# Ten projections of a 1-core Trainium2 kernel: from channel-major matmuls of 256 columns to token-major matmuls of 512

## The chip, the cores and the metric

One Trainium2 chip, one core. The metric is device time in microseconds of one launch. Three runs of the kernel before gave 1682.53, 1684.06 and 1685.83 us; the median is 1684.06 us. The profiled execution, one more run, took 1684.61 us.

## The reference, cut to what matters

Two stacked networks work on 256 tokens of width 1024, batch 1, all in float32. The first has two layers of feed-forward, three-branch mixer, feed-forward. The second is one layer: a mixer of a gated delta rule beside an S5 state-space model, cross attention on 256 memory tokens, a feed-forward. The parts that the change touches are the inputs of channel-wise operations:

```python
# first network, state-space branch, in each of two layers
xbc = (h @ w_in[l])[..., 2208:3232]                # 1024 channels
xbc = silu(causal_conv4(xbc) + conv_b)             # along the tokens
xs, b_in, c_in = split(xbc, [512, 768])            # into the chunked scan
# second network, mixer
proj = rmsnorm(h) @ w_in
q, k, v = split(silu(causal_conv4(proj[..., :1536])), 3)   # 512 each
u = proj[..., 2056:2568]                           # 512, input of the S5 scan
o = gated_delta_rule(l2norm(q) * 128**-0.5, l2norm(k), v, g, beta)
y = s5(u)
# second network, cross attention
k_mem = rmsnorm(mem) @ w_xk                        # 1024 channels
```

## The kernel before

Tokens come in two halves of 128 (`t`), the width in eight tiles of 128 (`k`). A normed input is held transposed, features on partitions and 256 tokens along the free axis, as a pair: a rounded high part `hi` and the rest `lo`, both fp32r. Each float32 product is three matmuls, which `mac` (lines 284 to 288) issues: high by high, high by low, low by high. The row norm of the input (`r`, one value a token) is applied after the product.

Weights stream through `wload` (line 158): a DMA from the SyncE queue into one of five stage tiles of 128x1024 (`NS`), a ScalarE cast into one of four `whi` tiles (line 165), a VectorE subtraction into one of four `wlo` tiles (line 166, `NW`). These run at the highest priority (`WPRIO`). One such tile is 512 KB.

There are two forms of projection. `lin_tok` (line 290) is token-major: 128 tokens of the input are stationary, 512 weight columns move, and the output has tokens on partitions, in one PSUM bank for each token half. `lin_ft` (line 309) is channel-major: 128 weight columns are stationary, the 256 tokens move, and the output has channels on partitions. What needs channels on partitions (a convolution along the tokens, the S5 scan, the keys) comes from `lin_ft`:

- `channels` in `mixer1` (line 563, two layers): eight tiles of 128 channels in two groups of four. VectorE multiplies two of them at a time with `rrow`, the norms spread along the free axis (line 572). Then follow `conv` (line 474: ScalarE scaling, three VectorE steps a channel tile), tanh and one more step.
- `proj_ft` in `mixer2` (line 1238): the same for k, q, v (in this order, each with its convolution and SiLU) and u.
- `mem_kv` (line 1336): eight tiles of memory keys, evacuated by ScalarE, then the memory values with `lin_tok`.

`r_rows` (line 487) makes `rrow`: two TensorE transposes of a broadcast column and a ScalarE copy. It is called once in each `mixer1` and once in `mixer2`.

The feed-forwards (`ffn`, line 369) already turn a token-major product without TensorE, in `flip` (line 267). VectorE transposes 32x32 blocks of `hb` (line 273), four DMAs write the blocks to a DRAM tile in their new places (line 277, 64 KB each), one DMA reads it back (line 279, 256 KB), and `split_evac` (lines 188 and 189) makes the fp32r pair. The tile `hb` and the landing tile `flipped` have one buffer each, `flip` and the DRAM tile two.

The order on each engine is the tile framework's: it simulates the program on a cost model and takes ready instructions by priority, which is program order moved by the `high_priority` blocks. All DMAs are issued from SyncE in the order of that plan, and an instruction that waits holds up those behind it on its engine. In `mixer1` the steps come in the order of `SEQ` (line 36): x is `channels`, u the gated MLP, q the attention heads, z the state-space gate, S the scan, A the attention, then gates and branches. The scan and the attention have a raised priority. In `mixer2` the delta rule (`delta`, line 1036) stands ahead of its place by `DPRIO`; `s5_scan` (line 980) and `mem_kv` come after it in the program, `s5_scan` in four chunks of 128 channels of u. A gate projection of the scan's output (`gT`) follows, then `lin_out` with the outputs of both.

Of the kernel before, what the change touches and what calls it, by code (L numbers as in the profile page):

```python
# [8 lines left out]
F32 = mybir.dt.float32  # L9
F32R = mybir.dt.float32r  # L10
I32 = mybir.dt.int32
AF = mybir.ActivationFunctionType
# [54 lines left out]
class Net:  # L67
# [198 lines left out]

    def flip(self, src, n, hi, lo, t):


        nc = self.nc  # L270
        w = n * 32
        r = self.A([512], "flip")[:, :4 * w]
        nc.vector.transpose(r, src)
        d = self.dram.tile([P, 4 * w], F32, name="flips", tag="flips")
        to = d.rearrange("(j c) (i e) -> i c j e", c=32, e=w)
        for i in range(4):
            nc.sync.dma_start(out=to[i], in_=r[i * 32:i * 32 + 32].rearrange("p (j e) -> p j e", e=w))
        raw = self.A([512], "flipped")[:, :4 * w]
        nc.sync.dma_start(out=raw, in_=d)
        tok = slice(t * P, (t + 1) * P)  # L280
        hi, lo = [z[:, :, tok].rearrange("p k (a b) -> p k a b", b=32) for z in (hi, lo)]
        self.split_evac(raw.rearrange("p (a k b) -> p k a b", k=n, b=32), hi, lo)

# [25 lines left out]
    def lin_ft(self, xT, w, c, out):  # L309

        hi, lo = xT
        n = len(w)
        cc = slice(c * P, (c + 1) * P)
        for k in range(n):
            wh, wl = w[k]
            self.mac(out, wh[:, cc], wl[:, cc], hi[k], lo[k], k == 0, k == n - 1)

    def wcols(self, src, n):
# [50 lines left out]
    def ffn(self, norm, w_in, w_out, scale, nxt, aside=None):  # L369
        nc = self.nc  # L370
        xT, r = norm["xT"], norm["r"]
        hh, hl = [], []
        for c in range(6):
            n = 512 if c < 5 else 256
            th = self.A([4, S], "hTh", F32R)
            tl = self.A([4, S], "hTl", F32R)
            ps = self.lin_tok(xT, w_in[c * 8:c * 8 + 4], 512)
            if c < 5:
                pg, pu = ps, self.lin_tok(xT, w_in[c * 8 + 4:c * 8 + 8], 512)
            else:  # L380
                pg, pu = [[p[:, i * n:(i + 1) * n] for p in ps] for i in range(2)]
            for t in range(2):
                sg = self.A([512], "sg")
                nc.scalar.activation(sg[:, :n], pg[t][:, :n], AF.Silu, scale=r[t])
                hb = self.A([512], "hb")[:, :n]
                nc.vector.scalar_tensor_tensor(hb, pu[t][:, :n], r[t], sg[:, :n], ALU.mult, ALU.mult)
                self.flip(hb, n // P, th[:, :n // P], tl[:, :n // P], t)
# [98 lines left out]

    def r_rows(self, r, pool):

        p = self.tp()
        for t in range(2):  # L490
            self.row_bcast(r[t], p[:, t * P:(t + 1) * P])
        o = pool.tile([P, S], F32, name="rrow")
        self.nc.scalar.copy(o, p[:, :S])
        return o

    def mixer1(self, l, norm, nxt):
        nc, a = self.nc, self.a
        v, act, pe = nc.vector, nc.scalar, nc.tensor
        tt, stt, ts = v.tensor_tensor, v.scalar_tensor_tensor, v.tensor_scalar
        lay = self.lay = Arena(self, 3072, "lay1")  # L500
        xT, r = norm["xT"], norm["r"]
# [61 lines left out]
        def channels():  # L563

            rrow = self.r_rows(r, lay)
            for g in range(2):
                xb = self.A([4, S], "xb")
                for c2 in range(2):
                    p = self.mm()
                    for c in range(2):  # L570
                        self.lin_ft(xT, self.wcols(a["m1_xbc"][l][g * 4 + c2 * 2 + c][None], P), 0, p[:, c * S:(c + 1) * S])
                    tt(xb[:, c2 * 2:c2 * 2 + 2], self._shape(p, [2, S]),
                       rrow[:, None, :].to_broadcast([P, 2, S]), ALU.mult)
                d = self.A([4, S], "xc")
# [634 lines left out]
    def mixer2(self, norm, nxt):  # L1209
        nc, a = self.nc, self.a  # L1210
        v, act, pe = nc.vector, nc.scalar, nc.tensor
        tt, stt, ts = v.tensor_tensor, v.scalar_tensor_tensor, v.tensor_scalar
        lay = self.lay = Arena(self, 2560, "lay2")
        alog = self.row(a["dn_a_log"], 4, "alog2")
# [21 lines left out]
        rrow = self.r_rows(r, lay)  # L1236

        def proj_ft(src, dst):
            for i in range(src.shape[0] // 2):
                p = self.mm()  # L1240
                for c in range(2):
                    self.lin_ft(xT, self.wcols(src[i * 2 + c][None], P), 0, p[:, c * S:(c + 1) * S])
                tt(dst[i // 2][:, (i % 2) * 2:(i % 2) * 2 + 2], self._shape(p, [2, S]),
                   rrow[:, None, :].to_broadcast([P, 2, S]), ALU.mult)

# [33 lines left out]
        for i in (1, 0, 2):  # L1279
            xb = self.A([4, S], "xb2")  # L1280
            proj_ft(a["m2_qkv"][i * 4:i * 4 + 4], [xb])
            d = self.A([4, S], f"qkv{i}")
# [4 lines left out]
        uT = self.A([4, S], "uT")  # L1287
        proj_ft(a["m2_u"], [uT])

# [46 lines left out]
    def mem_kv(self, xT):  # L1336
        nc, a = self.nc, self.a
        self.xk = [self.A([4, S], "xk") for _ in range(2)]
        for i in range(4):
            p = self.mm()  # L1340
            for c in range(2):
# [120 lines left out]


def _out_w(w, cols=COLS):

# [16 lines left out]
def _prep(inp):  # L1482
# [15 lines left out]
    for l in range(2):  # L1498
        wl = w[l]
        cqw.append(_blk(wl, 1024, 384, 2))  # L1500
        ckvw.append(_blk(np.concatenate([wl[:, 1408:1696], wl[:, 3232:3240]], axis=1), 0, 296, 2))
        xbc.append(np.concatenate([_blk(wl, 2208 + P * i, P, 8) for i in range(8)]))
        zz.append(_blk(wl, 1696, 512, 2))
# [23 lines left out]
    w = inp["w_in_2"][0]  # L1527
    o["m2_u"] = np.concatenate([_blk(w, 2056 + P * i, P, 8) for i in range(4)])
    o["m2_qkv"] = np.concatenate([_blk(w, P * i, P, 8) for i in range(12)])
    o["m2_z0"] = _blk(np.concatenate([w[:, 1536:1792], w[:, 2048:2056]], axis=1), 0, 264, 2)  # L1530
# [27 lines left out]
    o["mem"] = inp["mem_2"].reshape(2, P, D)  # L1558
    for k in "qk":
        o["x_" + k] = np.concatenate([_blk(inp[f"w_x{k}_2"][0], P * i, P, 8) for i in range(8)])  # L1560
    o["x_v"] = np.concatenate([_blk(inp["w_xv_2"][0], 512 * i, 512, 2) for i in range(2)])
# [37 lines left out]
```

## Time and profile before

| | before |
|---|---|
| median of three runs | 1684.06 us |
| lowest and highest | 1682.53 and 1685.83 us |
| profiled execution, its own time | 1684.61 us |
| its span in the profile | 1682.7 us |
| TensorE busy, matmuls | 1662.7 us, 9222 |
| VectorE busy | 1133.0 us |
| ScalarE busy | 902.6 us |
| moved by DMA | 321.92 MB |

Times in the trace are counted from the start of the span. "PE" is TensorE's matmuls, "PEld" its weight loads, "DVE" is VectorE, "ACT" ScalarE, "SPq" the SyncE queue that issues DMAs. The duration of a matmul overlaps that of the next. "mm", "mmm" and "chs" are PSUM banks; "xh" and "xl" are the pair of the normed input, "memh" and "meml" that of the memory.

### The profile page before, as it was taken

Reading aid. Unit: us, or ns where it says so; the run is one execution under the profiler, and the core shown is the slowest. Engines: PE = TensorE matmul, PEld = TensorE weight load, DVE = VectorE, ACT = ScalarE, POOL = GpSimd, SP = SyncE. Lnnn points to the kernel's source line nnn. Section 1 sums busy time; section 2 is a strip of 40 time slices with the busy share of each in tenths; the row PEclk is TensorE's granted clock in tenths of the full one; section 3 lists DMA queues with packets and bytes.
Section 4 is the critical chain, followed back from the end, with each engine's and each line's share of the span. In section 5 each row is a group of like instructions: output and inputs, shape, how many; then the busy total and the mean of one; then the engine's idle time right before and its main releaser. Section 6 shows DMA issues by size and latency. Waiting matters only on the chain.

```text
span 1682.7 us, 24668 instructions
## 1 busy us (share of the span) xinstructions
PE 1662.7 (99%) x9222; PEld 1423.0 (85%) x9222; DVE 1133.0 (67%) x1840; ACT 902.6 (54%) x1361; POOL 78.6 (5%) x73
## 2 busy tenths in 40 slices
PE   8999999999999999999999999999999999999998
PEld 6888898888888888888988888888899888888888
DVE  5665598657666556665896666799689746755664
ACT  5444467564544444544666545545476555654443
POOL 0000013000000000000130000000010100000000
PEclk9999999999999999999999999999999999999999
DMA  7787556444677757786664545767764224347872
GB/s 257 242 241 246 180 187 188 156 141 132 199 245 248 232 175 239 251 237 187 206 191 144 161 145 190 231 202 233 237 197 141 64 63 154 123 150 237 262 241 99
DMA packets 132744, 321.92 MB, mean 191 GB/s; under 512 B 24592, under 2 KB 52752, under 8 KB 132624
## 3 DMA queue, kind: packets, MB, share of 16 engines
q1 hardware_dynamic: 132624, 320.35, 60.7%
q8 instruction: 72, 1.18, 0.3%
q14 instruction: 48, 0.39, 0.1%
HBM read 304.82 MB, written 15.47 MB: 190 GB/s over the span
## 4 chain that ended last, share of the span: by engine, by line
PE 96%; DVE 1%; ACT 1%; issue 0%; DMA 0%; POOL 0%; SPq 0%; POOLq 0%; DVEq 0%; ACTq 0%
PE mm L287 28%; PE mm L286 28%; PE mm L288 28%; PE tp L206 1%; PE mmm L286 1%; PE mmm L288 1%; PE mmm L287 1%; PE ch L752 1%; PE chs L999 1%; PE ch L774 1%; PE tp L263 1%; PE ch L1137 0%; PE tp L636 0%; PE ch L715 0%; ACT whi L165 0%
## 5 line engine op out<-in xcount | busy, mean ns | idle before, releaser
L166 DVE TENSOR_TENSOR wlo<-stage,whi 128x1024 fp32r<-128x1024 f32 (+3 forms) x552 | 658.4, 1198 | 327.6 <-ACT whi L165 318.3
L165 ACT CAST whi<-stage 128x1024 fp32r<-128x1024 f32 (+3 forms) x552 | 567.3, 1034 | 452.4 <-PE mm L288 351.3
L287 PE MATMUL mm<-wlo,xh 128*128 128x512 f32 (+3 forms) x1264 | 485.5, 386 | 0.0
L288 PE MATMUL mm<-whi,xl 128*128 128x512 f32 (+4 forms) x1264 | 481.1, 385 | 0.0
L286 PE MATMUL mm<-whi,xh 128*128 128x512 f32 (+3 forms) x1264 | 472.4, 386 | 0.3 <-ACT xh L210 0.3
L287 PEld LDWEIGHTS mm<-wlo,xh 128*128 128x128 f32 x1264 | 237.8, 188 | 46.9 <-DVE wlo L166 1.6
L286 PEld LDWEIGHTS mm<-whi,xh 128*128 128x128 f32 x1264 | 237.3, 188 | 45.7 <-ACT xh L210 0.7
L288 PEld LDWEIGHTS mm<-whi,xl 128*128 128x128 f32 x1264 | 236.8, 188 | 44.7
L288 PE MATMUL mm<-whi,hTl 128*128 128x512 f32 (+1 forms) x484 | 179.0, 370 | 0.0
L287 PE MATMUL mm<-wlo,hTh 128*128 128x512 f32 (+1 forms) x484 | 179.0, 370 | 0.0
L286 PE MATMUL mm<-whi,hTh 128*128 128x512 f32 (+1 forms) x484 | 178.8, 371 | 0.0
L188 ACT CAST hTh<-flipped 128x512 fp32r<-128x512 f32 (+1 forms) x60 | 35.1, 585 | 160.0 <-DMA flipped<-flips 148.5
L174 POOL TENSOR_TENSOR small<-small,cst 128x1 f32<-128x1 f32 (+2 forms) x60 | 59.9, 1004 | 1154.5 <-DVE small L172 1142.4
L189 DVE TENSOR_TENSOR hTl<-flipped,hTh 128x512 fp32r<-128x512 f32 (+1 forms) x60 | 38.8, 647 | 99.6 <-ACT hTh L188 99.6
L288 PEld LDWEIGHTS mm<-whi,hTl 128*128 128x128 f32 x484 | 91.2, 188 | 15.5
L287 PEld LDWEIGHTS mm<-wlo,hTh 128*128 128x128 f32 x484 | 91.2, 189 | 15.3
L286 PEld LDWEIGHTS mm<-whi,hTh 128*128 128x128 f32 x484 | 91.2, 188 | 15.3
L286 PE MATMUL mm<-xh,whi 128*128 128x256 f32 x320 | 90.8, 285 | 1.2 <-ACT xh L210 1.2
L287 PE MATMUL mm<-xl,whi 128*128 128x256 f32 x320 | 90.7, 284 | 1.1 <-DVE xl L211 1.1
L288 PE MATMUL mm<-xh,wlo 128*128 128x256 f32 x320 | 89.9, 283 | 0.0
L287 PEld LDWEIGHTS mm<-xl,whi 128*128 128x128 f32 x320 | 61.3, 192 | 1.6 <-DVE xl L211 1.5
L286 PEld LDWEIGHTS mm<-xh,whi 128*128 128x128 f32 x320 | 61.1, 191 | 1.4 <-ACT xh L210 1.4
(525 smaller groups left out, 2009.9 us busy)
## 6 DMA issues: line engine op xcount, KB each, us to landing
stage<-in_ffn_in SPq DMA_DIRECT2D x176, 512.0 KB, 4.3
stage<-in_ffn_out SPq DMA_DIRECT2D x88, 512.0 KB, 4.5
stage<-in_m_g SPq DMA_DIRECT2D x48, 512.0 KB, 4.0
stage<-in_f_in SPq DMA_DIRECT2D x44, 512.0 KB, 4.4
flips<-flip SPq DMA_DIRECT2D x200, 64.0 KB, 3.4
flipped<-flips SPq DMA_DIRECT2D x50, 256.0 KB, 3.7
stage<-in_m_br SPq DMA_DIRECT2D x24, 512.0 KB, 3.5
stage<-in_m_out SPq DMA_DIRECT2D x24, 512.0 KB, 3.7
```

What stands on the lines that cost most here:

```text
L165: nc.scalar.copy(h, s)
L166: self.wsub = nc.vector.tensor_tensor(l, s, h.bitcast(F32), ALU.subtract).ins
L174: nc.gpsimd.tensor_tensor(r, m, self.mhalf[:, :n], ALU.pow)
L188: self.nc.scalar.copy(hi, ps)
L189: self.nc.vector.tensor_tensor(lo, ps, hi.bitcast(F32), ALU.subtract)
L206: nc.tensor.transpose(p[:, k, t * P:(t + 1) * P], x[t][:, (k0 + k) * P:(k0 + k + 1) * P], self.ident)
L263: nc.tensor.transpose(p[:, k * P:(k + 1) * P], src[:, k * P:(k + 1) * P], self.ident)
L286: mm(out, lh, rh, start=first, stop=False)
L287: mm(out, lh, rl, start=False, stop=False)
L288: mm(out, ll, rh, start=False, stop=last)
L752: pe.matmul(p3[:, i], qT[:96, b * hb + i, toks[t]], kT[:96, b * hb + i, :nk], start=True, stop=True)
L774: pe.matmul(p[:, h * 64:(h + 1) * 64], pT[kb][:, h], vv[kb][:, h], start=kb == 0, stop=kb == t)
```

## The change

Ten groups of 512 channels go from `lin_ft` to `lin_tok`. Each token half is evacuated by ScalarE, with the norm `r[t]` as a per-partition scale (the keys without it), turned by `flip`, and copied by ScalarE from the landing tile to its place in the channel-major output. `flip` now returns the turned tile; what the feed-forward did inside it is in `flip_T`. `r_rows` is gone, and with it 512 columns of each mixer's arena of small tensors. The host stores the weights of the ten groups in tiles of two k tiles by 512 columns instead of eight by 128, their columns reordered within a group by `_flipped_to`, so that the turn through 32x32 blocks leaves the channels in the old order. Weight bytes and weight tiles stay as many as before.

```diff
-    def flip(self, src, n, hi, lo, t):
+    def flip(self, src, w, rows=4):
         nc = self.nc
-        w = n * 32
-        r = self.A([512], "flip")[:, :4 * w]
+        n = rows * w
+        r = self.A([512], "flip")[:, :n]
         nc.vector.transpose(r, src)
-        d = self.dram.tile([P, 4 * w], F32, name="flips", tag="flips")
+        d = self.dram.tile([P, 512], F32, name="flips", tag="flips")[:32 * rows, :4 * w]
         to = d.rearrange("(j c) (i e) -> i c j e", c=32, e=w)
         for i in range(4):
             nc.sync.dma_start(out=to[i], in_=r[i * 32:i * 32 + 32].rearrange("p (j e) -> p j e", e=w))
-        raw = self.A([512], "flipped")[:, :4 * w]
+        raw = self.A([512], "flipped")[:32 * rows, :4 * w]
         nc.sync.dma_start(out=raw, in_=d)
+        return raw.rearrange("p (a k b) -> p a k b", a=4, b=32)
+
+    def flip_T(self, src, n, hi, lo, t):
+
         tok = slice(t * P, (t + 1) * P)
         hi, lo = [z[:, :, tok].rearrange("p k (a b) -> p k a b", b=32) for z in (hi, lo)]
-        self.split_evac(raw.rearrange("p (a k b) -> p k a b", k=n, b=32), hi, lo)
+        self.split_evac(self.flip(src, n * 32).rearrange("p a k b -> p k a b"), hi, lo)
...
+    def lin_flip(self, xT, src, out, r=None):
+
+        act = self.nc.scalar
+        ps = self.lin_tok(xT, src, 512)
+        for t in range(2):
+            z = self.A([512], "hb")
+            if r:
+                act.activation(z, ps[t], AF.Copy, scale=r[t])
+            else:
+                act.copy(z, ps[t])
+            z = self.flip(z, P).rearrange("p a k b -> p k a b")
+            act.copy(out[:, :, t * P:(t + 1) * P].rearrange("p k (a b) -> p k a b", b=32), z)
...
-        lay = self.lay = Arena(self, 3072, "lay1")
+        lay = self.lay = Arena(self, 2560, "lay1")
...
-            rrow = self.r_rows(r, lay)
             for g in range(2):
                 xb = self.A([4, S], "xb")
-                for c2 in range(2):
-                    p = self.mm()
-                    for c in range(2):
-                        self.lin_ft(xT, self.wcols(a["m1_xbc"][l][g * 4 + c2 * 2 + c][None], P), 0, p[:, c * S:(c + 1) * S])
-                    tt(xb[:, c2 * 2:c2 * 2 + 2], self._shape(p, [2, S]),
-                       rrow[:, None, :].to_broadcast([P, 2, S]), ALU.mult)
+                self.lin_flip(xT, a["m1_xbc"][l][g * 4:g * 4 + 4], xb, r)
...
-            proj_ft(a["m2_qkv"][i * 4:i * 4 + 4], [xb])
+            self.lin_flip(xT, a["m2_qkv"][i * 4:i * 4 + 4], xb, r)
...
-        proj_ft(a["m2_u"], [uT])
+        self.lin_flip(xT, a["m2_u"], uT, r)
...
-        for i in range(4):
-            p = self.mm()
-            for c in range(2):
-                self.lin_ft(xT, self.wcols(a["x_k"][i * 2 + c][None], P), 0, p[:, c * S:(c + 1) * S])
-            nc.scalar.copy(self.xk[i // 2][:, (i % 2) * 2:(i % 2) * 2 + 2], self._shape(p, [2, S]))
+        for i in range(2):
+            self.lin_flip(xT, a["x_k"][i * 4:i * 4 + 4], self.xk[i])
...
+def _flipped_to(w):
+
+    return w.reshape(w.shape[0], -1, 4, 4, 32).transpose(0, 1, 3, 2, 4).reshape(w.shape)
```

`r_rows` and `proj_ft` are deleted, the second mixer's arena goes from 2560 to 2048 columns, and `ffn` calls `flip_T` where it called `flip`.

## Rows read from the trace of the kernel before

**Rows 1.** The page: engines with share of the span, and the chain by engine.
```profile
PE 1662.7 (99%) x9222; PEld 1423.0 (85%) x9222; DVE 1133.0 (67%) x1840; ACT 902.6 (54%) x1361; POOL 78.6 (5%) x73
...
PE 96%; DVE 1%; ACT 1%; issue 0%; DMA 0%; POOL 0%; SPq 0%; POOLq 0%; DVEq 0%; ACTq 0%
```

**Rows 2.** Stretches: a feed-forward chunk; q, k, v, u; delta rule and scan.
```profile
core 0: us, PE busy (x) PEld busy (x) DVE busy (x) ACT busy (x) POOL busy (x), PEclk, DMA share, GB/s
...
1234.00:1282.00 48.00, 48.00 (x404) 48.00 (x403) 45.63 (x99) 30.12 (x48) 2.56 (x1) 1.00 0.60 188
1282.00:1412.00 130.00, 127.93 (x1333) 112.62 (x1331) 83.98 (x158) 74.11 (x134) 9.01 (x6) 1.00 0.28 86
...
90.00:111.60 21.60, 21.60 (x97) 17.87 (x96) 13.96 (x15) 10.65 (x13) 0.00 (x0) 1.00 0.83 253
```

**Rows 3.** TensorE in order of time (start, duration): feed-forward, 512 columns; state-space channels, 256.
```profile
90.02 0.39 PE L286 MATMUL mm<-whi,xh 128*128 128x512 f32 x1
...
110.88 0.39 PE L288 MATMUL mm<-whi,xl 128*128 128x512 f32 x1
...
220.07 0.28 PE L286 MATMUL mm<-xh,whi 128*128 128x256 f32 x1
...
224.15 0.28 PE L287 MATMUL mm<-xl,whi 128*128 128x256 f32 x1
```

**Rows 4.** Groups by form (busy us, mean ns | idle before): one line of three.
```profile
L286 PE MATMUL mm<-xh,whi 128*128 128x256 f32 x320 | 90.8, 285 | 1.2 <-ACT xh L210 1.2
...
L286 PE MATMUL mmm<-memh,whi 128*128 128x256 f32 x64 | 18.6, 291 | 0.0
```

**Rows 5.** TensorE in order of time around the two transposes of r_rows.
```profile
219.42 0.36 PE L286 MATMUL mm<-xh,whi 128*128 128x256 f32 x1
219.62 0.38 PE L472 MATMUL tp<-cst,small 128*128 128x128 f32 x2
...
219.96 0.28 PE L288 MATMUL mm<-xh,wlo 128*128 128x256 f32 x1
```

**Rows 6.** Groups by form: weight preparation, and the feed-forward's turn.
```profile
L166 DVE TENSOR_TENSOR wlo<-stage,whi 128x1024 fp32r<-128x1024 f32 x520 | 631.5, 1220 | 304.4 <-ACT whi L165 295.2 <-DMA flips<-flip 6.0 <-DMA flipped<-flips 0.3
L165 ACT CAST whi<-stage 128x1024 fp32r<-128x1024 f32 x520 | 543.6, 1052 | 426.7 <-PE mm L288 325.9 <-PE mm L287 33.8 <-issue 18.8
...
L273 DVE STREAM_TRANSPOSE flip<-hb 128x512 f32<-128x512 f32 x50 | 35.5, 710 | 1.4
...
L188 ACT CAST hTh<-flipped 128x512 fp32r<-128x512 f32 x50 | 31.0, 621 | 134.6 <-DMA flipped<-flips 123.0 <-DVE wlo L166 5.2 <-DMA stage<-in_ffn_in 3.9
```

**Rows 7.** Single tiles (ns min/median/max, first and last start).
```profile
L479 ACT ACTIVATE qkv<-xb,lay x12: 493/497/508, 1245.2 to 1273.8; 128x256 f32<-128x256 f32 x12
...
L1243 DVE TENSOR_TENSOR xb<-mm,lay x6: 631/685/692, 1243.9 to 1271.7; 128x512 f32<-128x512 f32 x6
...
L615 ACT ACTIVATE kv<-mm,small x8: 686/688/715, 261.6 to 872.4; 128x512 f32<-128x512 f32 x8
```

**Rows 8.** VectorE and ScalarE in order of time: two turns of a feed-forward chunk.
```profile
99.25 0.74 DVE L386 SCALAR_TENSOR_TENSOR hb<-mm,small,sg 128x512 f32<-128x512 f32 x1
...
108.69 0.62 ACT L188 CAST hTh<-flipped 128x512 fp32r<-128x512 f32 x1 [2.45 <-DMA flipped<-flips]
...
113.67 0.62 ACT L188 CAST hTh<-flipped 128x512 fp32r<-128x512 f32 x1 [1.30 <-DMA flipped<-flips]
```

**Rows 9.** Waits: total us, times, longest.
```profile
ACT hTh L188 <- DMA flipped<-flips: 148.5, 56, 7.3
```

**Rows 10.** u: its last matmul, the scan's first use, and the gate projection's input.
```profile
1282.93 0.28 PE L288 MATMUL mm<-xh,wlo 128*128 128x256 f32 x1
...
L991 ACT ACTIVATE s5u<-uT,cst x16: 736/752/776, 1281.3 to 1358.9; 128x256 f32<-128x256 f32 x16
...
L286 PE MATMUL mm<-gT,whi x16: 277/283/363, 1390.7 to 1400.8; 128*128 128x256 f32 x16
...
L189 DVE TENSOR_TENSOR gT<-uT,gT x1: 1226/1226/1226, 1383.5 to 1383.5; 128x1024 fp32r<-128x1024 f32 x1
```

More of the change, by code (lines that the diff above doesn't have):

```diff
@@ L386, in ffn @@
                 nc.vector.scalar_tensor_tensor(hb, pu[t][:, :n], r[t], sg[:, :n], ALU.mult, ALU.mult)
-                self.flip(hb, n // P, th[:, :n // P], tl[:, :n // P], t)
+                self.flip_T(hb, n // P, th[:, :n // P], tl[:, :n // P], t)
             for k in range(n // P):
@@ L485, in conv @@
                                        ALU.mult, ALU.add)
[L487 to L494, printed above, removed]
     def mixer1(self, l, norm, nxt):
@@ L1212, in mixer2 @@
         tt, stt, ts = v.tensor_tensor, v.scalar_tensor_tensor, v.tensor_scalar
-        lay = self.lay = Arena(self, 2560, "lay2")
+        lay = self.lay = Arena(self, 2048, "lay2")
         alog = self.row(a["dn_a_log"], 4, "alog2")
@@ L1235, in mixer2 @@
             rh.append(h)
-        rrow = self.r_rows(r, lay)
-        def proj_ft(src, dst):
-            for i in range(src.shape[0] // 2):
-                p = self.mm()
-                for c in range(2):
-                    self.lin_ft(xT, self.wcols(src[i * 2 + c][None], P), 0, p[:, c * S:(c + 1) * S])
-                tt(dst[i // 2][:, (i % 2) * 2:(i % 2) * 2 + 2], self._shape(p, [2, S]),
-                   rrow[:, None, :].to_broadcast([P, 2, S]), ALU.mult)
         zg = [lay.tile([P, 4, P]) for _ in range(2)]
@@ L1338, in mem_kv @@
         self.xk = [self.A([4, S], "xk") for _ in range(2)]
-        for i in range(4):
-            p = self.mm()
-            for c in range(2):
-                self.lin_ft(xT, self.wcols(a["x_k"][i * 2 + c][None], P), 0, p[:, c * S:(c + 1) * S])
-            nc.scalar.copy(self.xk[i // 2][:, (i % 2) * 2:(i % 2) * 2 + 2], self._shape(p, [2, S]))
+        for i in range(2):
+            self.lin_flip(xT, a["x_k"][i * 4:i * 4 + 4], self.xk[i])
         self.xv = [self.A([D], "xv") for _ in range(2)]
@@ L1501, in _prep @@
         ckvw.append(_blk(np.concatenate([wl[:, 1408:1696], wl[:, 3232:3240]], axis=1), 0, 296, 2))
-        xbc.append(np.concatenate([_blk(wl, 2208 + P * i, P, 8) for i in range(8)]))
+        xbc.append(np.concatenate([_blk(_flipped_to(wl[:, 2208:3232]), 512 * i, 512, 2) for i in range(2)]))
         zz.append(_blk(wl, 1696, 512, 2))
@@ L1527, in _prep @@
     w = inp["w_in_2"][0]
-    o["m2_u"] = np.concatenate([_blk(w, 2056 + P * i, P, 8) for i in range(4)])
-    o["m2_qkv"] = np.concatenate([_blk(w, P * i, P, 8) for i in range(12)])
+    o["m2_u"] = _blk(_flipped_to(w[:, 2056:2568]), 0, 512, 2)
+    o["m2_qkv"] = np.concatenate([_blk(_flipped_to(w[:, :1536]), 512 * i, 512, 2) for i in range(3)])
     o["m2_z0"] = _blk(np.concatenate([w[:, 1536:1792], w[:, 2048:2056]], axis=1), 0, 264, 2)
@@ L1558, in _prep @@
     o["mem"] = inp["mem_2"].reshape(2, P, D)
-    for k in "qk":
-        o["x_" + k] = np.concatenate([_blk(inp[f"w_x{k}_2"][0], P * i, P, 8) for i in range(8)])
+    o["x_q"] = np.concatenate([_blk(inp["w_xq_2"][0], P * i, P, 8) for i in range(8)])
+    o["x_k"] = np.concatenate([_blk(_flipped_to(inp["w_xk_2"][0]), 512 * i, 512, 2) for i in range(2)])
     o["x_v"] = np.concatenate([_blk(inp["w_xv_2"][0], 512 * i, 512, 2) for i in range(2)])
```

## The prediction

> **What bounds it now.** I read the page first: TensorE is busy for 99% of the span, and the chain that ended last runs on it for 96% [rows 1]. A busy TensorE can still hide waits, so next I cut the span into stretches [rows 2]. In the feed-forward stretch and in the q, k, v, u stretch of the second mixer TensorE is never idle; over the delta rule and S5 scan it lacks 2.1 of 130 us. VectorE is the runner-up where convolutions run: 45.6 of 48 us. ScalarE has 30.1 of those 48. So the time is TensorE's issue time plus little else, and what counts is the distance from one matmul's start to the next, not the mean duration, which overlaps.
>
> That distance is in the order of time [rows 3]. With 512 moving columns, 93 starts run from 90.02 to 110.88: 20.86/92 = 0.2267 us. With 256, 35 starts run from 220.07 to 224.15: 4.08/34 = 0.1200 us. Half the columns cost 53% of the time, so two halves cost 0.2400 where one whole costs 0.2267.
>
> **The change, part by part.**
>
> *Matmuls.* The moved projections are ten groups of 512 channels: two in each of the two state-space layers, q, k, v, u, and two of memory keys. Today a group is 4 channel tiles x 8 k tiles x 3 = 96 matmuls of 256 columns. The counts agree [rows 4]: 320 a line, of which 64 are the query projection, which stays, and 64 for the memory keys; 256 + 64 = 320 = ten groups of 32. Afterwards a group is 2 token halves x 8 x 3 = 48 matmuls of 512. Then 96 x 0.1200 = 11.52 becomes 48 x 0.2267 = 10.88: 0.64 us a group, **6.4 us** in ten. All of it is on the path where TensorE is full.
>
> Here a rule speaks against the change. The rows price the narrow matmul above half of the wide one. The Trainium skill, "TensorE: Matmul & The Clock Gate", section "Back-to-back issue gap", gives the isolated gap as columns/2.4 ns plus 2.5 ns, 109.2 and 215.8 ns, so a group would save only 96 x 0.1092 - 48 x 0.2158 = 0.12 us and ten 1.2 us; it adds that streams with weight loads deviate from this, and the rows here do, at 0.1200 and 0.2267.
>
> *The row of norms.* r_rows goes, three times. Each put two transposes into the stream: from 219.42 to 219.96 two steps took 0.54 instead of 0.24 [rows 5]. That is 0.3 us each, **0.9 us** in three, on the path. Its ScalarE copy goes too; ScalarE isn't the bound, so nothing for that.
>
> *VectorE.* A group loses two multiplies from PSUM (0.685 each [rows 7]) and gets two transposes (0.710 [rows 6]): +0.05 us, nothing. The two key groups had no such multiply and gain 1.4 us each, in a stretch where VectorE has 84 of 130 [rows 2]. But the q, k, v, u work of 45.6 us now has to fit a stretch shortened by 4 x 0.64, so VectorE is at 100% there and the last convolution slips a few us. Behind it waits only the value part of the delta rule. The weight subtraction keeps its place in front by priority.
>
> *ScalarE.* Before, a q, k or v group costs four casts (4.2), four conv scalings (4 x 0.497) and one function over 1024 columns (about a cast, 1.05): 7.25 us [rows 6, 7]. The change adds two evacuations (0.688 each, from the nearest row, a scaled copy of the same shape out of PSUM) and two copies out of the turned tile (0.621): 9.9 us, in a group of 10.88. That alone fits. The question is the wait: in the feed-forward the copy stands at the head of ScalarE until its read lands, 148.5 us in 56 waits, 2.65 each [rows 9]. Queued behind it are the weight casts, behind those the subtractions, then TensorE. Lower bound of the cost: nothing, as the feed-forward bears such waits with TensorE never idle [rows 2]; no gain is possible, because nothing that a cast waits for goes away. Upper bound: 9.9 + 5.3 = 15.2, 4.3 beyond the group; the u group without convolution 4.2 + 2.6 + 5.3 = 12.1, 1.2 beyond. Casts run three weight tiles ahead (four slots): 3 x 12 x 0.2267 = 8.2 us of cover. In the second mixer 3 x 4.3 + 1.2 - 8.2 = 5.9, in each state-space layer 2 x 4.3 - 8.2 = 0.4: **6.7 us** at most. I take **1.5**, near the feed-forward row, since a wait that other ready work precedes is shorter.
>
> *SyncE and DMA.* Each of 20 turns adds four writes, which wait for the transpose, and one read, which waits for the writes to land; the weight loads stand behind them on SyncE. In the feed-forward one pair of turns takes from 99.25 to 113.67 + 0.62: 15.0 us, and the two copies out stand 5.0 us apart (108.69 and 113.67) [rows 8], because there is one landing tile. Two turns thus need 10 us of a group's 10.88: they keep up, barely. Traffic: a feed-forward chunk of 21.6 us with one pair of turns moves 253 GB/s at a share of 0.83 [rows 2]; twice the turns per time adds 1.05 MB per 21.8 us, 48 GB/s: about 300 GB/s, an estimate, near a full queue. Loads will land later there; five staged tiles (13 us) cover that. Nothing taken.
>
> *Lateness.* A channel tile now needs both token halves and a turn of 15 us. State-space channels are wanted well after the two projections that follow them; the memory keys are wanted in the next block; k, q and v have u behind them. Only u is wanted at once: the S5 scan masks it from 1281.3 on, while its last matmul starts at 1282.93 [rows 10]. Its matmuls would end 2.6 us earlier, near 1280.4, plus 15.0: 1295.4, 14.1 late. TensorE meanwhile has the memory keys (10.88 x 2) and the front of the delta rule, so it stays full at first. Bounds: nothing, if the scan's four chunks close up; if they keep their spacing, the gate projection comes 14.1 us later, less the 6.0 that its input waits for TensorE today (1383.5 + 1.2 to 1390.7 [rows 10]): 8.1. I take **0.5**, because that stretch is held by TensorE's order, with matmuls of the memory keys put between the scan's.
>
> Weights reordered on the host, smaller arenas and the wider DRAM tile issue nothing: no cost.
>
> **Sum:** -6.4 - 0.9 + 1.5 + 0.5 = -5.3 us. The profiled execution took 1684.6 (span 1682.7 and 1.9 around it), so 1679.3; the median shown is 0.55 lower, so **1679**. A measurement of this kernel can tell about 0.2%, 3.4 us, from no change.
>
> **Rivals.**
>
> 1. *ScalarE paces the projections* through copies that wait at its head. For it: 2.65 us a wait, twice as dense as today. Against it: the feed-forward shows no idle TensorE. Price 6.7: -6.4 - 0.9 + 6.7 + 0.5 = -0.1, so 1684: no change.
>
> 2. *The late u leaves a hole* at the end of the second mixer: memory keys and values are used up early, and the scan and gate projection come last, with TensorE idle. For it: u is turned last of the four, and today the scan starts before u's last matmul. Against it: full TensorE in between. Only the state-space part is then kept, -(4 x 0.64 + 0.6) = -3.2, plus 8.1: +4.9, 1689. It decides as soon as the scan's chunks are not moved up by more than half of the 14 us. With part of rival 1 as well it is 1690 or more.
>
> 3. *The narrow matmul is no dearer per column in sustained flow* (its 0.1200 being local to that stretch). Then only the 0.9 goes and 2.0 is added: 1685. Against it: the stretch of q, k, v and u has 404 matmuls in 48.00 us [rows 2], 0.119 each, so the distance holds there too. By the page of the Trainium skill named above this case would be 1.2 us quicker still.
>
> **Chances.** Forecast, 1675 to 1682: 0.54. Rival 1: 0.20. Rival 3: 0.02. Rival 2 with its mixture: 0.24. So faster by over 0.2%: 0.54; within: 0.22; slower: 0.24. The range reaches from the whole 7.3 with nothing given back (1677, less 2 for the spread of runs) to rival 2: 1675 to 1690. The likeliest case alone is 1675 to 1682.
>
> **What would show it.** Right: 960 narrow matmuls gone, 480 wide ones at 0.227 us; TensorE without idle time in the channel stretches; six norm transposes gone. Rival 1: casts late with "DMA flipped" before them, then matmuls released by VectorE's subtraction. Rival 2: TensorE idle between the last memory value matmul and the mixer's output projection, released by the scan. The forecast is wrong if TensorE's busy time falls by 6 us and the span does not.

## The result, and the profile after

The changed kernel takes 1709.8 us in the median, the kernel before 1684.7 beside it: ratio 1.0146, 95% interval 1.0133 to 1.0159. That is 25 us slower, where 5 us faster was forecast and 1690 was the end of the range. The profiled execution has a span of 1709.8.

The page after, engines and chain (against [rows 1]):

```profile
PE 1673.0 (98%) x8736; PEld 1404.8 (82%) x8736; DVE 1138.6 (67%) x1844; ACT 929.5 (54%) x1399; POOL 81.4 (5%) x73
...
PE 85%; DVE 4%; ACT 4%; DMA 3%; issue 2%; SPq 0%; POOLq 0%; POOL 0%; ACTq 0%; DVEq 0%
```

9222 matmuls became 8736: 480 fewer, and the six transposes of the norm rows. The work that was to go is gone. But the chain that ended last now leaves TensorE for 15% of the span, before for 4%. TensorE in order of time, in a state-space layer's channels:

```profile
228.97 0.39 PE L291 MATMUL mm<-wlo,xh 128*128 128x512 f32 x1
...
235.32 0.39 PE L290 MATMUL mm<-whi,xh 128*128 128x512 f32 x1
```

28 distances in 6.35 us are 0.2268 each, the forecast's 0.2267 [rows 3]. Worked out from these distances, the matmuls save what they were to save, 7.3 us with the norm rows, and 32.4 us were lost beside it (34.4 by the two profiled executions, whose spans are 27.1 apart). The stretches show where (columns as in [rows 2]); first the changed kernel, both state-space layers and the second mixer with its cross attention:

```profile
220.00:240.00 20.00, 18.98 (x85) 15.09 (x84) 13.87 (x51) 9.26 (x18) 4.49 (x4) 1.00 0.70 216
240.00:260.00 20.00, 19.11 (x91) 15.06 (x89) 17.74 (x33) 18.86 (x29) 1.54 (x2) 1.00 0.70 211
260.00:280.00 20.00, 19.21 (x95) 16.11 (x95) 20.00 (x47) 16.07 (x25) 3.26 (x2) 1.00 0.63 187
...
400.00:420.00 20.00, 18.80 (x84) 14.97 (x83) 11.24 (x20) 8.52 (x20) 0.00 (x0) 0.83 0.19 54
...
840.00:860.00 20.00, 18.05 (x75) 13.33 (x73) 14.34 (x39) 9.14 (x14) 0.00 (x0) 1.00 0.77 227
860.00:880.00 20.00, 18.86 (x98) 16.33 (x99) 17.68 (x37) 17.07 (x27) 2.41 (x2) 1.00 0.63 181
880.00:900.00 20.00, 18.90 (x87) 15.10 (x85) 20.00 (x51) 15.49 (x24) 8.52 (x5) 1.00 0.69 207
1000.00:1040.00 40.00, 38.20 (x193) 30.77 (x192) 28.99 (x44) 18.77 (x35) 0.00 (x0) 1.00 0.38 116
...
1280.00:1320.00 40.00, 39.84 (x200) 33.08 (x199) 35.69 (x64) 34.77 (x58) 1.92 (x1) 1.00 0.78 239
1320.00:1360.00 40.00, 36.44 (x275) 28.95 (x275) 31.81 (x63) 29.70 (x47) 3.29 (x3) 0.96 0.47 141
1360.00:1400.00 40.00, 37.81 (x492) 32.13 (x491) 20.22 (x44) 20.49 (x39) 0.00 (x0) 0.99 0.18 54
1400.00:1440.00 40.00, 37.31 (x347) 31.84 (x348) 23.69 (x39) 19.51 (x33) 2.02 (x2) 0.93 0.20 56
1440.00:1480.00 40.00, 37.84 (x252) 34.99 (x251) 26.04 (x40) 21.43 (x34) 1.08 (x2) 0.96 0.52 168
1480.00:1520.00 40.00, 38.18 (x225) 34.06 (x224) 25.20 (x41) 22.92 (x44) 0.00 (x0) 0.96 0.37 118
```

The kernel before, those of the same stretches in which TensorE was not full; in all the others of them it was, and the granted clock is 1.00 in each:

```profile
400.00:420.00 20.00, 19.66 (x100) 16.09 (x99) 13.59 (x19) 9.21 (x13) 0.00 (x0) 1.00 0.34 106
...
1000.00:1040.00 40.00, 39.66 (x199) 32.80 (x198) 28.06 (x39) 19.45 (x29) 1.08 (x2) 1.00 0.51 166
...
1320.00:1360.00 40.00, 39.45 (x466) 34.67 (x467) 24.13 (x45) 19.07 (x30) 3.59 (x1) 1.00 0.18 54
...
1400.00:1440.00 40.00, 36.21 (x206) 30.57 (x205) 27.60 (x43) 22.90 (x37) 2.46 (x3) 1.00 0.46 148
1440.00:1480.00 40.00, 38.18 (x275) 35.80 (x274) 27.26 (x44) 23.22 (x41) 0.00 (x0) 1.00 0.42 132
```

TensorE's idle time rises by 3.6 us in the first layer (3.9 against 0.3), 5.7 in the second (6.0 against 0.3) and 6.4 in the last six stretches (12.6 against 6.2): 15.7. Beside that stands the clock, which is at half in five stretches (windows inside them, columns as above):

```profile
405.80:412.50 6.70, 6.70 (x25) 5.91 (x25) 1.53 (x4) 0.51 (x2) 0.00 (x0) 0.50 0.26 81
1330.80:1334.10 3.30, 3.30 (x12) 2.66 (x11) 0.86 (x1) 3.29 (x5) 0.00 (x0) 0.50 0.53 206
1399.10:1405.80 6.70, 6.08 (x14) 4.88 (x15) 0.00 (x0) 2.03 (x5) 0.00 (x0) 0.50 0.01 2
1460.50:1463.80 3.30, 3.30 (x16) 3.14 (x15) 0.51 (x2) 0.00 (x0) 0.00 (x0) 0.50 0.00 0
1487.80:1491.10 3.30, 3.30 (x18) 3.30 (x17) 1.95 (x4) 0.06 (x1) 0.00 (x0) 0.50 0.71 258
```

TensorE is busy for 22.7 us of them at half speed: some 11 us lost. That fits TensorE's busy time, which rose (1662.7 to 1673.0 us) though 486 matmuls went. 15.7 and 11 are 27 of the 34.4; where the rest lies isn't shown. Executions of the changed kernel differ in this: two took 1707.9 and 1708.1 us at a mean granted clock of 0.996 and 0.995, two 1711.5 (the profiled one) and 1713.5 at 0.992 and 0.991.

Nor is all of it the turn's. In the control with nothing turned (the last under "The chain started earlier") the clock stands at half twice, in the same place of the second network, which the kernel before passed at 1.00:

```profile
1437.60:1441.00 3.40, 3.40 (x17) 3.40 (x17) 0.11 (x1) 0.58 (x1) 0.00 (x0) 0.50 0.00 0
1464.90:1468.30 3.40, 3.40 (x18) 3.40 (x18) 1.66 (x4) 0.70 (x3) 0.00 (x0) 0.50 0.59 218
```

So the two windows at 1460.5 and 1487.8, 3.3 of the 11 us, aren't shown to be the change's.

How a stall arises shows ScalarE in order of time in the first layer's channels:

```profile
225.78 0.69 ACT L329 ACTIVATE hb<-mm,small 128x512 f32<-128x512 f32 x1
...
228.52 1.06 ACT L165 CAST whi<-stage 128x1024 fp32r<-128x1024 f32 x1
236.40 0.62 ACT L333 COPY xb<-flipped 128x512 f32<-128x512 f32 x1 [6.82 <-DMA flipped<-flips]
236.92 1.04 ACT L165 CAST whi<-stage 128x1024 fp32r<-128x1024 f32 x1
...
240.29 0.62 ACT L333 COPY xb<-flipped 128x512 f32<-128x512 f32 x1 [1.74 <-DMA flipped<-flips]
```

The copy out of the turned tile stands at ScalarE's head for 6.82 us, and the next weight cast behind it: none starts between 228.52 and 236.92. TensorE has used up its cast weights by then:

```profile
238.01 0.73 PE L290 MATMUL mm<-whi,xh 128*128 128x512 f32 x2 [0.49 <-ACT whi L165]
239.28 0.50 PE L291 MATMUL mm<-wlo,xh 128*128 128x512 f32 x1 [0.53 <-DVE wlo L166]
```

And SyncE's queue, with the turns of the same group:

```profile
228.06 1.81 SPq L277 DMA_DIRECT2D flips<-flip  x4
...
230.68 0.30 SPq L277 DMA_DIRECT2D flips<-flip  x1
233.07 0.34 SPq L279 DMA_DIRECT2D flipped<-flips  x1
233.46 1.43 SPq L277 DMA_DIRECT2D flips<-flip  x3
```

Three of the second turn's writes wait behind the first turn's read, which waits for its own writes to land. First evacuation to second copy: 225.78 to 240.91, 15.1 us; the forecast had 15.0 from [rows 8].

The second thing to see is lateness. The state-space scan's first operand and the attention's outputs (ns min/median/max, first and last start), before:

```profile
L687 DVE TENSOR_TENSOR xdd<-xs,small x1: 683/683/683, 298.7 to 298.7; 128x512 f32<-128x512 f32 x1
...
L776 DVE TENSOR_TENSOR ao<-ch,small x4: 416/422/425, 355.2 to 401.2; 128x256 f32<-128x256 f32 x4
```

and after:

```profile
L689 DVE TENSOR_TENSOR xdd<-xs,small x1: 684/684/684, 309.7 to 309.7; 128x512 f32<-128x512 f32 x1
...
L778 DVE TENSOR_TENSOR ao<-ch,small x4: 418/422/425, 367.3 to 410.3; 128x256 f32<-128x256 f32 x4
```

The scan starts 11.0 us later, and the attention, which the plan puts behind it, ends 9.1 later. There TensorE idles 1.2 us for 0.3 and has the half clock, in the stretch 400 to 420; as I read it, few projections are left there to put between.

### The profile page after: what moved, and what is told of

Read it like the earlier page. It is cut to its first block, busy times and chain, and to the rows that moved or that the text cites. A ratio compares the mean times of both kernels' runs of the same rounds, so it can differ in the third digit from the quotient of the medians.

```text
span 1709.8 us, 23902 instructions
## 1 busy us (share of the span) xinstructions
PE 1673.0 (98%) x8736; PEld 1404.8 (82%) x8736; DVE 1138.6 (67%) x1844; ACT 929.5 (54%) x1399; POOL 81.4 (5%) x73
## 4 chain that ended last, share of the span: by engine, by line
PE 85%; DVE 4%; ACT 4%; DMA 3%; issue 2%; SPq 0%; POOLq 0%; POOL 0%; ACTq 0%; DVEq 0%
PE mm L291 26%; PE mm L290 25%; PE mm L292 25%; ACT whi L165 1%; DVE wlo L166 1%; DMA flipped<-flips 1%; PE tp L206 1%; DMA flips<-flip 1%; PE chs L1001 1%; PE ch L776 1%; PE ch L754 1%; DMA stage<-in_m_uv 1%; PE tp L263 0%; DVE qkv L501 0%; PE tp L638 0%
## 5 line engine op out<-in xcount | busy, mean ns | idle before, releaser
L291 PE MATMUL mm<-wlo,xh 128*128 128x512 f32 (+3 forms) x1392 | 535.1, 386 | 3.5 <-DVE wlo L166 3.5
L292 PE MATMUL mm<-whi,xl 128*128 128x512 f32 (+4 forms) x1392 | 531.2, 386 | 0.0
L290 PE MATMUL mm<-whi,xh 128*128 128x512 f32 (+3 forms) x1392 | 518.9, 387 | 2.3 <-ACT whi L165 1.6
L291 PEld LDWEIGHTS mm<-wlo,xh 128*128 128x128 f32 x1392 | 261.6, 188 | 56.7 <-DVE wlo L166 6.8
L292 PEld LDWEIGHTS mm<-whi,xl 128*128 128x128 f32 x1392 | 260.8, 188 | 49.4
L188 ACT CAST hTh<-flipped 128x512 fp32r<-128x512 f32 (+1 forms) x60 | 35.2, 587 | 137.8 <-DMA flipped<-flips 134.1
L273 DVE STREAM_TRANSPOSE flip<-hb 128x512 f32<-128x512 f32 (+1 forms) x80 | 54.0, 675 | 6.6 <-ACT hb L329 5.0
L210 ACT ACTIVATE xh<-tp,small 128x256 fp32r<-128x256 f32 x72 | 31.1, 472 | 21.1 <-PE tp L206 16.8
L403 DVE SCALAR_TENSOR_TENSOR hb<-mm,small,sg 128x512 f32<-128x512 f32 (+1 forms) x60 | 42.0, 700 | 0.0
L211 DVE SCALAR_TENSOR_TENSOR xl<-tp,small,xh 128x256 fp32r<-128x256 f32 x72 | 32.0, 478 | 12.6 <-ACT xh L210 12.4
L401 ACT ACTIVATE sg<-mm,small 128x512 f32<-128x512 f32 (+1 forms) x60 | 38.9, 649 | 1.4 <-PE mm L292 1.2
```

The lines of the kernel that those rows point to most:

```text
L188: self.nc.scalar.copy(hi, ps)
L211: nc.vector.scalar_tensor_tensor(lo, p[:, i], g, hi.bitcast(F32), ALU.mult, ALU.subtract)
L290: mm(out, lh, rh, start=first, stop=False)
L291: mm(out, lh, rl, start=False, stop=False)
L292: mm(out, ll, rh, start=False, stop=last)
```

## The experiments

All are timed against the kernel before on the same chip; ratios with 95% intervals.

**One part at a time.** In each, the parts not named keep their channel-major projection and the row of norms:

```
-    self.lin_flip(xT, a["m2_u"], uT, r)
+    self.lin_cols(xT, a["m2_u"], uT, rrow)   # as proj_ft of the kernel before
```

*Only the state-space channels.*

> Only the state-space channels of the two layers are projected token-major and turned; q, k, v, u and the memory keys are as before. Theory A (the loss sits where the trace shows it: about +10 us in each state-space layer, against 3.2 us of matmul and norm-row gain, plus +8 to +10 in the second mixer): the first weight load of q, k, v came 16.0 us later after the change, so this kernel is 1684.7 + 16 = 1701 us, within 3 us. Theory B (the state-space part is fine by itself; what the layers lose depends on the q, k, v, u, key part): 1684.7 - 3.2 = 1681.5. Theory C (any change to this packed order loses some us by reordering, whatever its size): 1690 or so, like the next kernels.

1697.7 us, 1.0079 (1.0059 to 1.0098): 13 us slower, nearest to theory A, just under its 1701 within 3.

*Only u.*

> Only the S5 input u is projected token-major and turned; all else as before. Theory A (u late by a whole turn, the scan's first matmul and gate projection late, and TensorE's granted clock halved after the idle time): the second mixer's share, 25.1 - 16.0 = 9 us, comes from u: 1684.7 + 9 = 1694, within 3. Rival D (lateness of u is covered by other work; the second mixer's loss is q, k and v's, with ScalarE standing at the copies): 1684.7 - 0.6 = 1684.

1684.7, 1.0000 (0.9990 to 1.0009): nothing. Rival D.

*Only the memory keys.*

> Only the memory keys are projected token-major and turned; all else as before. Theory A (a turned tile that is wanted a block later costs nothing but its own copy): 1684.7 - 1.3 = 1683.4. Theory C (any change of the order costs some us): 1690. Rival E (four copies standing at the head of ScalarE cost what they do in the state-space layer): the two key groups are as many as one layer has, so + 8: 1692.

1691.4, 1.0044 (1.0030 to 1.0059): 6.7 us slower, between C and E. TensorE in order of time shows the longest hole:

```profile
1464.19 1.09 PE L1412 MATMUL tp<-cst,xpr 128*128 128x128 f32 x4 [3.63 <-DVE xpr L1408]
...
1466.55 0.41 PE L290 MATMUL ch<-xks,xq 128*128 128x256 f32 x1
1466.77 0.41 PE L291 MATMUL ch<-xks,xq 128*128 128x256 f32 x1
```

This is the cross attention, some 120 us behind the last copy of a turned key (1338.2). The planner wrote ScalarE's order anew: two weight casts, xq and xpT now stand between the second and the third exponential. TensorE idles 3.63 us, and the matmuls after it start 0.22 apart where they start 0.12 apart at full clock. That is not all: from 1320 to 1400 TensorE idles 2.2 us for 0.6 in the kernel before, in the delta rule.

*All but u.*

> The changed kernel with u alone put back to the channel-major projection with its row of norms (r_rows once more). Theory A: the state-space part stays (+16), the second mixer's loss goes and q, k, v and the keys give 5 x 0.64 = 3.2: 1684.7 + 16 - 3.2 = 1697.5. Rival D (the loss is q, k and v's): the second mixer keeps it, 1709.

1708.5, 1.0140 (1.0116 to 1.0164): rival D again; the 1.3 us less than the changed kernel are within the noise. 23.8 less 13.0 and 6.7 leaves 4.1 for q, k and v, if the parts add up.

**ScalarE's head of the line.** The copy goes to GpSimd, or gets two landing tiles:

```
-            act.copy(out[:, :, t * P:(t + 1) * P]..., z)
+            nc.gpsimd.tensor_copy(out[:, :, t * P:(t + 1) * P]..., z)
---
-    sg=2, hb=1, flip=2, flipped=1,
+    sg=2, hb=1, flip=2, flipped=2,
```

> The changed kernel, but the copy out of the turned tile is GpSimd's and no longer ScalarE's, so no cast of a weight stands behind it. Theory A (casts that stand behind that copy cost the state-space layers their time: stalls ended by a cast or its subtraction come to about 5 us in each layer more than before): two layers and half as much for q, k, v and keys come back, 12 us: 1709.8 - 12 = 1698. Theory C (the loss lies in the order that the planner writes for places far from the turns: the layer's attention end, the scan's end, the cross attention): those stalls stay, 1705 or more, or move elsewhere. Rival F (the copy on ScalarE is hidden anyway and GpSimd's is slower): 1710 or more.

1701.1, 1.0086 (1.0060 to 1.0111): 8.7 us back (10 by the ratios), between A's figure and C's bound, nearer to A. But the stalls that A speaks of went only in part: TensorE's idle time from 200 to 300 and 820 to 920, the two layers' channels, fell from 6.9 to 4.8 us, and the clock stands at half for some 10 us instead of 23. What stands at ScalarE's head now is the convolution's first tap:

```profile
243.85 2.08 ACT L519 ACTIVATE xc<-xb,lay 128x256 f32<-128x256 f32 x4 [6.01 <-POOL xb L333]
```

> The changed kernel with two landing tiles instead of one, so that the read of the second turn of a group doesn't wait until the copy out of the first has ended. Theory A (ScalarE stands for the second turn's read because there is one landing tile; 1.7 us at the second turn, 6.8 at the first): the smaller part of the waits goes, 20 x 1 to 1.7 at most, some 5 us of them on the path: 1705. Rival G (the wait is the chain of transpose, writes and read itself, not the tile): no change, 1709.8.

1718.5, 1.0186 (1.0159 to 1.0213): 7 to 9 us slower still (by the ratios, by the medians). A's part of it and G both missed. The tile serves the feed-forwards too, whose waits rose from 134.1 us in 57 to 183.2 in 59:

```profile
ACT hTh L188 <- DMA flipped<-flips: 183.2, 59, 5.3
```

In the first layer the second copy still starts 3.9 us behind the first (235.18 and 239.09, in the changed kernel 236.40 and 240.29), and its writes still stand behind the first turn's read on SyncE.

The same with the keys alone turned:

> Only the memory keys turned, with two landing tiles. The kernel of the earlier experiment with the keys alone lost 6.7 us, of which the trace shows 5.4 in the cross attention 80 us later, where ScalarE has two weight casts, xq and xpT between the second and the third exponential, then TensorE waits 3.8 us at half the granted clock. Here the program order on ScalarE has all four exponentials together again, as before the change. Theory C (that order is the cost): 1684.7 - 1.3 + 1.3 = 1684.7, within 1.5. Rival E (the turning of the keys is the cost): still 1691.

1694.8, 1.0053 (1.0036 to 1.0070). The cross attention is whole again (its transposes' wait is gone), yet no time came back: two landing tiles serve the feed-forwards too, from 1080 to 1180 TensorE now idles 2.2 us where it was full before, and from 1320 to 1400 it idles 2.7. So theory C as I had put it, one order in one place, falls. (The 80 us of the expectation count from the memory values; from the keys it is 120.)

**Fewer or other transfers.** One hop from SBUF to SBUF, or the read on another queue:

```
-            z = self.flip(z, P).rearrange("p a k b -> p k a b")
+        for i in range(4):
+            for j in range(4):
+                nc.sync.dma_start(out=out[j*32:j*32+32, :, i*32:i*32+32], in_=r[i*32:i*32+32, j*P:(j+1)*P]...)
---
-        nc.sync.dma_start(out=raw, in_=d)
+        nc.gpsimd.dma_start(out=raw, in_=d)
```

> The changed kernel, but the turned 32x32 blocks go by 16 transfers straight from the transposed tile into the place where the channels are wanted, with runs of 128 bytes: no write to DRAM and read back, no landing tile, no copy by ScalarE. Theory A (latency of the turn and ScalarE's copy behind it pace the projections): the waits go, the copies' 20 x 0.62 too, and the state-space layers get their 10 us back, the rest half: 1695. Theory C: 1705 or more. Rival H (runs of 128 bytes and 320 issues on SyncE are slow and hold the weight loads behind them): 1715 or more.

1745.6, 1.0345 (1.0313 to 1.0377): rival H, and worse. SyncE's issues of one line (ns min/median/max):

```profile
L341 SPq DMA_DIRECT2D xb<-flip x224: 585/599/1397, 228.2 to 1351.7; - x112
```

16 of 0.6 us are 9.6 a turn, 19 a group, and a group's matmuls take 10.9.

> The copy out on GpSimd, and the read back of the turned tile is issued from GpSimd's queue too, so SyncE's queue no longer stands until the four writes have landed, with the next turn's writes and the weight loads behind it (a second turn took 14.5 us from its evacuation to its copy, the first 10.5). Theory J (SyncE's in-order queue makes the turns slow, and shorter turns end the waits): 1701 - 5 = 1696. Theory A alone (it is what stands on ScalarE that counts, and the turn remains longer than the planner's order allows for): 1701 less 2 at most.

1720.2, 1.0199 (1.0184 to 1.0214): 19 us slower than with GpSimd's copies alone. All 70 reads moved, the feed-forwards' too, and from issue to landing they now take 4.6 us for 3.6 in the changed kernel. Both theories missed.

> Both together: copy and read on GpSimd, and the convolution behind the seventh (state-space layers) or fifth (second mixer) later cast. Theory A and J add up: 1701 - 6 - 3 = 1692. Theory C: unchanged 1701, or moved elsewhere.

1712.3, 1.0167 (1.0131 to 1.0204): the read's loss again; both theories missed.

**The convolution behind a later cast:**

```
+    self.late.append((len(self.wdma) + N1, lambda: conv_late(g, xb)))   # run in wload, behind that cast
```

> The copy out on GpSimd as before, and the convolution that follows (ScalarE's first tap, VectorE's other taps, the function) is put on ScalarE behind the cast of a later weight tile: the ninth after the group's own in the state-space layers, the sixth in the second mixer. Nothing on ScalarE then waits for a turn with weight casts behind it. Theory A (head of the line on ScalarE, whichever instruction stands there: in the experiment with GpSimd's copies it was the convolution's first tap, 6.01 us): the 240 to 275 and 840 to 880 stalls fall from some 4.5 to 1.5 us each: 1701 - 6 = 1695. Theory C (order elsewhere): unchanged, 1701, or moved elsewhere. Rival I (the convolutions become late and the scans behind them stand): over 1704.

1697.8, 1.0069 (1.0054 to 1.0084): 3 us better than GpSimd's copies alone, half of what A says. The edit did only half its work: in its trace the tap still stands 5.9 us at ScalarE's head in the first layer.

> Only the state-space channels turned, copy on GpSimd, convolution behind the ninth later cast. The same part with the copy on ScalarE was 13 us slower than before. Theory A: the layers' stalls by late casts go, and the saved matmul time shows: 1684.7 - 3.2 + 2 x 1.5 = 1684.5. Theory C (the end of the layers is written in another order whatever the turns do: some 3 us in each layer, and more at half clock): 1690.

1697.5, 1.0067 (1.0051 to 1.0083): C is the nearer of the two figures; both missed. The scan starts at 308.9 and the attention's last output at 409.4, as late as in the changed kernel. But the run doesn't decide between them: here too the tap stands 5.5 us at ScalarE's head, and TensorE idles 2.8 and 2.9 us in the layers' channels.

**The chain started earlier:**

```
+        channels()
         pas = self.lin_tok(xT, a["m1_cq"][l], 384)
         pbs = self.lin_tok(xT, a["m1_ckv"][l], 296)
```

> The changed kernel with one thing moved: in each state-space layer the two channel groups are projected ahead of the q and kv compressions (48 matmuls of 384 and 48 of 296 columns, some 14 us) instead of behind them. All operations stay. Theory K (lateness: the turned channels are ready some 10 us later, so the state-space scan starts at 308 instead of 297 and the attention behind it ends at 410 instead of 401, where no other matmuls are left to put between; the head of ScalarE's line matters less): the end of each layer loses its holes and the half clock, and the scan starts before 300: 2 x 2.5 + 3.4 = 8 us back: 1702. Theory A (casts behind a turn's copy on ScalarE pace the projections): the turns stand on ScalarE all the same: 1708 or more.

1702.6, 1.0106 (1.0091 to 1.0121): 7.2 us back, K's figure. The tiles of its first layer:

```profile
L711 DVE TENSOR_TENSOR xdd<-xs,small x1: 683/683/683, 303.0 to 303.0; 128x512 f32<-128x512 f32 x1
...
L800 DVE TENSOR_TENSOR ao<-ch,small x4: 418/421/424, 362.2 to 403.1; 128x256 f32<-128x256 f32 x4
```

6.7 of the 11.0 us of the scan's lateness and 7.2 of the attention's 9.1 are gone, and with them the layer's half clock. The move isn't clean: the longest wait for a turn on ScalarE fell there from 6.8 to 2.4 us too, since other work of ScalarE lies between. The stretches (columns as above) show that this weighs more: both layers' channels, then both layers' ends.

```profile
200.00:300.00 100.00, 99.52 (x513) 86.06 (x512) 81.36 (x200) 70.20 (x112) 22.08 (x15) 1.00 0.65 200
820.00:920.00 100.00, 99.75 (x519) 86.10 (x518) 83.54 (x204) 74.36 (x124) 22.10 (x15) 1.00 0.65 200
...
390.00:420.00 30.00, 28.52 (x147) 23.17 (x146) 20.04 (x33) 13.04 (x27) 0.00 (x0) 1.00 0.33 103
...
1000.00:1040.00 40.00, 38.19 (x188) 30.55 (x187) 26.21 (x39) 21.73 (x41) 0.00 (x0) 1.00 0.42 140
```

TensorE's idle time in the channels is 0.7 us, in the changed kernel 6.9. At the ends it is 1.5 and 1.8, there 1.2 and 1.8: the holes that K said would go are still there, and only the first layer's half clock (6.7 us, 3.4 lost) went. So K's figure came out, but most of what the layers got back are the stalls that A speaks of.

> The channels first and the copy out on GpSimd. Theory K and A both at work: 1701 (GpSimd's copies alone) - 8 = 1693. Theory A alone: 1701.

1695.9, 1.0052 (1.0032 to 1.0073): 6.7 us better than the channels first alone, 5.2 better than GpSimd's copies alone. The two edits add up nearly: 13.9 us back together, 7.2 and 8.7 alone.

> As the one before, and in the second mixer k, q and v are projected ahead of the two parts of the gate z (264 and 256 columns, some 12 us). Theory K: the delta rule's chain starts as early as before the change, the holes and the half clock at 1320 to 1420 go (some 6 us): 1693 - 6 = 1687 or less, the first version that comes near the kernel before. Theory A: as the one before.

1696.0, 1.0072 (1.0055 to 1.0089): no gain, where K had 6 us. TensorE's idle time from 1240 to 1440 fell from 8.9 to 6.0 us, but from 1320 to 1440 the granted clock is 0.94 for 0.97. So an earlier start of k, q and v doesn't bring the second mixer's time back; whether their lateness has a part in it stays open.

> Control: the kernel before the change with the channels ahead of the compressions, nothing turned. Theory K: the chain was covered already, so an earlier start is worth little: 1682 to 1685. If this alone gives 5 us or more, what the moved channels win in the turned kernel isn't the turn's lateness.

1687.3, 1.0012 (1.0002 to 1.0021): the move alone gains nothing (it is 2.4 us slower, with the clock at half twice for 3.4 us), so what it gives the turned kernel is the turn's loss.

**What remains.** The keys put back in the version with channels first and copies on GpSimd; and, with q, k, v back too, the attention ahead of the scan:

```
-SEQ = "u q z S A g0 b0 g2 g1 b2 b1"
+SEQ = "u q z A S g0 b0 g1 g2 b1 b2"
```

> The kernel with channels first and copies on GpSimd, with the memory keys alone put back to the channel-major projection. Theory L (each turned part of the second mixer costs by itself what it cost alone; the keys 6.7 us): 1695.9 - 6.7 = 1689. Rival M (the second mixer loses what it loses as soon as any of its chain is disturbed; k, q and v do that too): 1695 or more.

1693.8, 1.0047 (1.0033 to 1.0060): 2 us better, within the two intervals, not 6.7. The parts of the second mixer don't add up; nearer to M.

> State-space channels and u turned (k, q, v and the keys as before the change), channels first, copies on GpSimd, and in each state-space layer the attention, which needs no channel, ahead of the state-space scan in the order of priorities, with its branch ahead of the scan's. Theory K (the layer's end is set by the chain of scan and then attention, which started some 5 us later even with the channels first, and TensorE has no matmuls left at its end): the 2.3 us of holes at each layer's end go: 1684.7 - 3.8 + 2 x 1 = 1683, a version that is a little better than before or equal. Rival N (the scan, now last, leaves the same holes at the end): 1687 to 1690.

1709.4, 1.0142 (1.0121 to 1.0163): far beyond rival N. The scan as the last chain leaves a longer hole than the attention:

```profile
404.20 0.66 PE L263 MATMUL tp<-cst,y 128*128 128x128 f32 x2 [5.91 <-DVE y L759]
```

No version beat the kernel before; u alone equals it.

## Why the prediction was wrong, point by point

*Matmuls and norm rows: right.* 0.2268 measured for 0.2267, all 480 and the six transposes gone. The Trainium skill, "TensorE: Matmul & The Clock Gate", section "Back-to-back issue gap", gives 215.8 ns for an isolated 512 columns and some 131 ns for a sustained stream with weight loads. The new stream agrees with neither: with its weight loads it stays at the 0.2267 of the old one, so the rows were the right price.

*Traffic: no cost seen.* The channels' stretches move 181 to 227 GB/s, not the 300 estimated. Ahead of each layer's turns a weight cast does wait for its load, 2.1 and 2.0 us, while TensorE is full; whether that thins the cover behind it wasn't tested. *SyncE* was costed only by the pair of turns' 15.0 us; that the second turn's writes queue behind the first turn's read is part of those 15, and moving the read away cost more than it gave. The prediction put the distance of the two copies down to the one landing tile; with two it stayed at 3.9 us.

*ScalarE: right mechanism, wrong size.* This was rival 1, and its marks are all there: casts late, "DMA flipped" before them, matmuls released by the subtraction. I took 1.5 us and gave 6.7 as the upper end, from a mean wait of 2.65 in the feed-forward; here the wait was 6.82, near the longest one in [rows 9], 7.3. The upper end put 5.9 into the second mixer and 0.4 into each state-space layer. The trace has it the other way round: TensorE idles 2.7 and 4.2 us in the layers' channels, ended by late casts, the subtractions behind them and ScalarE's evacuations, and 0.2 us from 1240 to 1320, where q, k, v and u are projected. So this term is 6.9 us of idle time, without what the clock adds to it. The step that failed is "a wait that other ready work precedes is shorter": the cover of 8.2 us of cast weights was counted once a layer, and a turn takes 10.6 from its evacuation to its copy (225.78 to 236.40). That ScalarE's head is the cause is borne out by two edits that left it freer, GpSimd's copies (8.7 us back, with the convolution's tap still 6.01 in the same place) and the channels first (the 6.9 down to 0.7).

*Lateness: a second step that failed* is "State-space channels are wanted well after the two projections that follow them", costed at nothing. They were wanted: the plan puts scan and attention one behind the other to the layer's end, 103 us from 298.7 to 401.6, with projections as filler. Eleven us later at its head were 9.1 later at its end. There TensorE idles 1.2 us in the first layer and 1.8 in the second, for 0.3 in each before, and has the half clock once for 6.7 us: some 6 us together, by the trace. Starting the channels earlier gave 7.2 us back in all, but it left these holes and cleared ScalarE's head as well; how much is lateness, beyond the 3.4 of the half clock, isn't shown.

*u: the 0.5 was right, its rival wrong.* Turned alone, u is as late as forecast (the scan's first use starts at 1297.9; forecast 1295.4, before 1281.3), and the gate projection starts 4.8 us later (1395.5 for 1390.7); that costs 0.0 us. With all ten groups turned the first use is at 1327.2, and putting u back gives 1.3, within the noise. The loss has rival 2's sign, but not its mechanism.

*The keys and k, q, v: wrong.* "Wanted in the next block" is true, and the keys alone still cost 6.7 us. In that run most of the loss was not near them: a planner's order that fell otherwise some 120 us later, then half clock. Two landing tiles removed that place and the loss appeared elsewhere, and putting the keys back in the version with channels first and copies on GpSimd gave 2 at most. Which edit of the second mixer costs what stays open; that each loses time by a reshuffled order is shown in one place only.

*The clock: not in the prediction at all.* It stood at half in five stretches, some 11 us, more than any term of my sum; 3.3 of them, in two stretches, appear with nothing turned as well.

## What to carry to other kernels

A turn through memory is paid at the head of the in-order engine that picks it up: take the longest wait of its kind, not the mean, and move the pick-up to an idle engine or start the projection earlier. In a kernel whose bound engine is 99% busy, find the chains that the filler hides, and price a step's delay against the filler left at the chain's end, not against the next thing in program order; this second advice is argued here more than shown. When an edit helps, look in the trace for which idle time went: the figure of a theory can come out by another one's mechanism. Where a planner writes the order, any edit may move holes to places far from it; measure each part alone before summing.

## What the runs showed of the hardware

A hole can cost more than itself: after TensorE stood still for 3.63 us in the keys' run, and after 1.1 us idle in pieces from 400 to 405.7 in the changed kernel, the granted clock was at half. In the changed kernel 512-column starts then lay 0.43 apart, for 0.23 [rows 3]:

```profile
405.91 0.63 PE L290 MATMUL mm<-whi,ybT 128*128 128x512 f32 x1
406.34 0.63 PE L291 MATMUL mm<-wlo,ybT 128*128 128x512 f32 x1
```

Yet the kernel before idles 3.8 us between 1400 and 1440 and keeps 1.00, and the control with nothing turned idles 3.8 us there and has 0.97. What decides it wasn't tried. Issues have a price on their own queue: 0.60 us each for a 128-byte-run transfer on SyncE, and a read issued from GpSimd's queue took 1 us longer to land (4.6 for 3.6).
